# One layer of a hybrid encoder on one core: the weight sums of the output projection are made beside the first three attention steps instead of the last eight

## The chip, the core and the metric

The kernel runs on one core of one Trainium2 chip. A core has a matmul engine (TensorE, in the profile PE, with its weight loads as PEld), three engines for elementwise work (VectorE, DVE; ScalarE, ACT; GpSimd, POOL) and SyncE (SP), which issues nearly all DMAs here, in the order in which they are written. Each engine works through its own queue in order. The metric is the time of one execution in microseconds.

## What is computed

One layer works on 2048 tokens of width 1024 in float32. It has three parts, each with an RMS norm before and after and a residual: token mixing, cross-attention into 256 memory tokens, and a SwiGLU network. Token mixing is what matters here:

```python
z = u @ w_in                       # 1024 -> 2816 columns
qa, ka, va, qh, fh, ih, gh = jnp.split(z, IN_SPLITS, axis=-1)
ya = swa_with_sinks(qa, ka, va, sinks)      # sliding window attention, 8 heads
yh = hgrn2(qh, fh, ih, gh, lb, onorm)       # gated linear recurrence, 4 heads
y = jnp.concatenate([ya, yh], axis=-1) @ w_out
h = h + rms_norm(y, g_mix_post)
```

## The kernel before

**Precision.** Each float32 operand of a large product is split into a rounded high part and the rest, and a product is three matmuls (high by high, high by low, low by high; `mm3`, L156 to L158, and `products`, L1122 to L1124). The split is `split2`: the high part on ScalarE (L985) or GpSimd (L987), the low one on VectorE (L988).

**Seven products for eight.** Large products are cut into 2 x 2 blocks and made with seven block products (`seven`). For that, four sums and differences of the blocks of the moving operand are needed. For the output projection this operand is `w_out`. Its sums are made ahead of time and stored in a DRAM tensor, `out_s`, and read back as tiles `row` when the projection begins. `sums` sets that up, and the generator `combined` does it: for each of two halves of a block and for each of four keys it loads one or two blocks of `w_out` (L75, by `load`), into tiles `u` or `x` of the pool `io`, yields three times, combines them on VectorE (`put`, L1032), stores the result (L78, by `store`), and yields once more. In each half, key 5 combines an `x` into a `u`; key 7 another `x` into a new `u`, key 6 a third `x` into the same `u` once its first store has landed, and key 4 subtracts this `u` from a fourth `x`. A load of the upper rows of `w_out` takes two DMAs of 64 partitions each. There are 33 calls of `next` to the end of the generator.

**The stage around the change.** `mix` first projects the first 1024 tokens (`in_first`), and then runs three generators in turn, one step of each at a time:

- `in_proj`, L682, makes the input projection of the second 1024 tokens, one tile of 128 columns per step: 48 matmuls of 128 x 512 into banks `psg`, from weights `raw`, split into `whi` and `wlo`, with the result `z` stored to `z_d`. After the columns of a forget gate `decays` works on tiles `x` and `u` of the same pool.
- `swa` does the attention of 128 tokens per step: `swa_front` loads queries (`qd`, twice two halves), keys (`kr`) and values (`vr`) from `z_d`, splits them (`qs`, `kh` and `kl`, `vst`), multiplies (L803, L804), takes the softmax's minimum on VectorE (L808, `w_mn`), the exponential on ScalarE (L812) and scales on VectorE (L823); one step later `swa_back` transposes the result (L837), splits it (`pth`, `ptl`), multiplies by the values (L846, L847) and stores `ys` to `y_d`.
- `hgrn` does the recurrence of 128 tokens per step, in three stages over three steps, with loads `k`, `qq`, `kk`, `v` and `sg` from `z_d`; `on` (L933) is its normed output, which TensorE transposes (L941).

The first loop has nine steps (NPB + 1) with all three. The second has the remaining eight steps of `swa`, with `in_proj` but without `hgrn`, whose second half comes later, beside the products that fold the cross-attention's weights (`fold_cross`). Before the change the sums stand in this second loop: one `next` ahead of it and four per step.

**What sets the order.** The program is traced in the order of these calls; a scheduler then orders each engine's instructions from that, with its own estimate of when each could start, and pools set which tile waits for which. So a moved call also changes the order of its neighbours. Pools: `u` has 2 buffers, `x` 3, `raw` 3, `qd` 2, `kr` and `vr` 1.

Of the kernel before, what the change touches and what calls it, by code (L numbers as in the profile page):

```python
# [48 lines left out]
class Layer:  # L49
# [144 lines left out]
    def mix(self):  # L194
        tc, I = self.tc, self.I
        kw = dict(reuse_waits="tile")
        with contextlib.ExitStack() as left:
            def pool(name, at, **k):
                return at.enter_context(tc.tile_pool(name=name, bufs=1, **k, **kw))

            self.mc = pool("mc", left)
            self.r_x = self.cst.tile([P, NT], F32, name="r_x")
            with (
                tc.tile_pool(name="t1", bufs=3, **kw) as self.ts,
                tc.tile_pool(name="t2", bufs=3, **kw) as self.tb,
                tc.tile_pool(name="s1", bufs=2, side="right", **kw) as self.st_pool,
                contextlib.ExitStack() as at,
            ):
                self.banks(at, "ps1", **MOST)
                self.raws = 3  # L210
                u = self.in_first()
            self.banks(left, "ps2", **FOUR)
            self.hg = pool("hg", left)
            self.wp = pool("wp", left)
            self.io = pool("io", left)
            with tc.tile_pool(name="sw", bufs=1, side="right", **kw) as self.sw:
                self.zero_tiles()
                swa = self.swa(range(NT), lambda n: "st" if n < NPB else "sth")
                hgrn = self.hgrn(range(NPB), "h")
                cols = self.in_proj(1, u)  # L220
                next(cols)
                for _ in range(NPB + 1):
                    next(swa)
                    next(hgrn)
                    next(cols)
                for _ in hgrn:
                    pass
                self.out_sums, side = self.sums("out_s", self.w_out, 4, lambda: self.io_tile("u"), lambda: self.io_tile("x"))
                side = side()
                next(side)  # L230
                pairs = self.hgrn(range(NPB, NT), "gt")
                for i, _ in enumerate(swa, NPB + 2):
                    next(cols)
                    if i == NT + 1 - 0:
                        next(pairs)
                    for _ in range(4):
                        next(side, None)
                for _ in cols:
                    pass
            phases = self.phases(self.jobs(), None, lambda: self.io_tile("z"))  # L240
            with tc.tile_pool(name="xp", bufs=1, side="right", **kw) as self.xp:
                fold = self.fold_cross()
                for _ in range(2):
                    next(fold)
                for i, _ in enumerate(pairs, 1):
                    for _ in range(2):
                        next(fold)
                    if 2 <= i < 10:
                        next(phases)
                for _ in fold:  # L250
                    pass
            left.close()
            with (
                tc.tile_pool(name="t3", bufs=3, **kw) as self.ts,
                tc.tile_pool(name="t4", bufs=3, **kw) as self.tb,
                tc.tile_pool(name="s3", bufs=2, side="right", **kw) as self.st_pool,
                contextlib.ExitStack() as at,
            ):
                self.banks(at, "ps3", **MOST)
                self.raws = 4  # L260
                for _ in phases:
                    pass
# [1497 lines left out]
```

## Time and profile before

| what | us |
|---|---|
| median of three runs | 2584.37 |
| the three runs | 2583.25, 2584.37, 2588.23 |
| the profiled execution, as timed | 2585.97 |
| its span, first to last instruction | 2584.3 |
| first column of `in_proj` begins | 268 |
| last `out_s` store issued | 530 |
| first `out_s` read back | 782 |

The profile is one execution. An instruction's row names its line, engine, operation and tiles (out<-in, buffer numbers left out). A line can be that of a helper, so that loads are all on L75 and stores on L78; there the tile's name tells them apart. A wait row reads: who waited, on which line, for whom, the sum in us, how often, the longest. Times within the span count from its first instruction. A matmul of 512 columns is shown with some 390 ns but the next one starts before it has ended, so PE's busy time counts the union.

### The profile page before, as it was taken

What the parts mean: (1) busy time and instruction counts of PE and PEld (TensorE: products, weight loads), DVE (VectorE), ACT (ScalarE), POOL (GpSimd) and SP (SyncE); (2) the same over time, 40 slices, a digit from 0 to 9 for tenths busy, and PEclk for the clock granted to TensorE, in tenths of its full rate; (3) what the DMA queues carried; (4) which work ended last, traced back from release to release, by engine and by line L of the source; (5) the groups of instructions that cost most, each with busy time, mean ns of one, the idle gap of its engine ahead of it and who ended that gap; (6) DMA issues with size and microseconds to landing.
All of it is one profiled execution on the core that took longest, in us unless ns stands there. A gap on an engine that the chain in (4) does not pass through costs nothing.

```text
span 2584.3 us, 34943 instructions
## 1 busy us (share of the span) xinstructions
PE 2540.1 (98%) x12326; PEld 2126.7 (82%) x12326; DVE 1762.3 (68%) x2791; ACT 1262.6 (49%) x2643; POOL 427.2 (17%) x612
## 2 busy tenths in 40 slices
PE   9999999999999999999999999999999999999998
PEld 8888888878998778888778888888888888888786
DVE  7785588887556778688875655576666557564666
ACT  5563466565555566465563333344333335443543
POOL 4231334321302232212300000000000000000022
PEclk9999999999999999999999999999999999999999
DMA  6445755765887886666973622253565434576888
GB/s 188 147 163 171 203 165 159 231 193 175 245 296 278 297 278 219 217 214 205 325 245 118 207 90 74 82 204 122 182 202 186 155 109 167 180 219 173 249 223 217
DMA packets 361616, 502.10 MB, mean 194 GB/s; under 512 B 20832, under 2 KB 249184, under 8 KB 361440
## 3 DMA queue, kind: packets, MB, share of 16 engines
q1 hardware_dynamic: 355392, 477.84, 56.2%
q0 software_dynamic: 6048, 22.02, 4.7%
q8 instruction: 97, 1.59, 0.2%
q14 instruction: 79, 0.65, 0.1%
HBM read 333.07 MB, written 166.72 MB: 193 GB/s over the span
## 4 chain that ended last, share of the span: by engine, by line
PE 77%; DMA 7%; issue 6%; DVE 4%; ACT 4%; POOL 1%; SPq 1%; POOLq 0%; DVEq 0%; ACTq 0%
PE psm L1122 21%; PE psm L1123 21%; PE psm L1124 21%; PE psg L158 2%; PE psg L156 2%; PE psg L157 2%; PE pss L1381 1%; DMA row<-y_d 1%; ACT T L985 1%; DMA y_d<-sg 1%; ACT junk L1476 1%; DMA x<-in_w_out_dram 1%; DMA h1t_d<-row 1%; DMA raw<-in_wo_x_dram 0%; SPq L75 0%
## 5 line engine op out<-in xcount | busy, mean ns | idle before, releaser
L1122 PE MATMUL psm<-T,S 128*128 128x512 f32 x2680 | 1037.9, 392 | 13.5 <-ACT part L1137 7.9
L1123 PE MATMUL psm<-T,S 128*128 128x512 f32 x2680 | 1043.5, 390 | 2.3 <-DVE T L988 2.2
L1124 PE MATMUL psm<-T,S 128*128 128x512 f32 x2680 | 1031.1, 390 | 4.8 <-DVE S L988 4.8
L1122 PEld LDWEIGHTS psm<-T,S 128*128 128x128 f32 x2680 | 503.5, 188 | 124.2 <-ACT part L1137 8.8
L1124 PEld LDWEIGHTS psm<-T,S 128*128 128x128 f32 x2680 | 503.8, 188 | 111.1 <-DVE S L988 6.5
L1123 PEld LDWEIGHTS psm<-T,S 128*128 128x128 f32 x2680 | 503.9, 188 | 107.0 <-DVE T L988 4.5
L985 ACT ACTIVATE S<-sum 128x512 fp32r<-128x512 f32 (+1 forms) x330 | 198.6, 618 | 363.2 <-PE psm L1124 269.3
L988 DVE TENSOR_TENSOR S<-sraw,S 128x512 fp32r<-128x512 f32 (+1 forms) x315 | 214.2, 687 | 220.8 <-ACT S L985 206.3
L988 DVE TENSOR_TENSOR S<-sum,S 128x512 fp32r<-128x512 f32 (+1 forms) x388 | 260.3, 679 | 45.9 <-ACT S L985 30.3
L1137 ACT ACTIVATE part<-psm 128x512 f32<-128x512 f32 x285 | 168.7, 596 | 239.8 <-PE psm L1124 219.7
L985 ACT ACTIVATE S<-sraw 128x512 fp32r<-128x512 f32 (+1 forms) x268 | 165.2, 617 | 101.0 <-PE psm L1124 92.3
L1505 POOL DMA_DIRECT2D row<-y_d x28 | 25.5, 911 | 1111.1 <-DMA sraw<-hid_d 955.0
L988 DVE TENSOR_TENSOR T<-row,T 128x1024 fp32r<-128x1024 f32 (+1 forms) x112 | 132.2, 1192 | 43.9 <-ACT T L985 43.5
L1476 ACT ACTIVATE junk<-row 128x512 f32<-128x512 f32 x160 | 99.7, 624 | 60.3 <-DVE row L1498 31.2
L157 PE MATMUL psg<-u,whi 128*128 128x512 f32 x320 | 127.8, 399 | 0.0
L158 PE MATMUL psg<-u,wlo 128*128 128x512 f32 x320 | 127.1, 397 | 0.0
L156 PE MATMUL psg<-u,whi 128*128 128x512 f32 x320 | 127.0, 397 | 0.0
L985 ACT ACTIVATE T<-row 128x1024 fp32r<-128x1024 f32 (+1 forms) x112 | 113.9, 1031 | 23.6 <-DMA row<-d_s 8.5
L987 POOL TENSOR_SCALAR S<-sum 128x512 fp32r<-128x512 f32 x58 | 54.1, 934 | 296.3 <-PE psm L1124 248.5
L1642 DVE TENSOR_TENSOR row<-psm,part 128x512 f32<-128x512 f32 x66 | 43.7, 687 | 68.2 <-PE psm L1124 68.2
L1651 DVE TENSOR_TENSOR part<-psm,part 128x512 f32<-128x512 f32 x66 | 43.8, 687 | 62.9 <-PE psm L1124 62.8
L1691 DVE TENSOR_TENSOR row<-psm,part 128x512 f32<-128x512 f32 x72 | 49.0, 688 | 52.8 <-PE psm L1124 52.8
(363 smaller groups left out, 3699.7 us busy)
## 6 DMA issues: line engine op xcount, KB each, us to landing
sraw<-in_w_gate_dram SPq DMA_DIRECT2D x44, 512.0 KB, 3.7
sraw<-in_w_up_dram SPq DMA_DIRECT2D x44, 512.0 KB, 3.7
hid_d<-row SPq DMA_DIRECT2D x44, 512.0 KB, 2.7
h_d<-row SPq DMA_DIRECT2D x32, 512.0 KB, 5.0
y_d<-row SPq DMA_DIRECT2D x32, 512.0 KB, 3.3
sraw<-hid_d SPq DMA_DIRECT2D x32, 512.0 KB, 4.7
row<-y_d POOLq DMA_DIRECT2D x28, 512.0 KB, 6.3
sraw<-in_w_in_dram SPq DMA_DIRECT2D x44, 256.0 KB, 3.6
```

Of the source, the lines that this page charges most:

```text
L156: nc.tensor.matmul(ps, ah, bh, start=(i == 0), stop=False)
L157: nc.tensor.matmul(ps, ah, bl, start=False, stop=False)
L158: nc.tensor.matmul(ps, al, bh, start=False, stop=(i == n - 1))
L985: self.nc.scalar.activation(hi, raw, AF.Copy)
L987: self.nc.gpsimd.tensor_scalar(hi, raw, 1.0, 1.0, ALU.mult, ALU.mult)
L988: self.nc.vector.tensor_tensor(lo, raw, f32(hi), ALU.subtract)
L1122: nc.tensor.matmul(ps, s[:, 0, k, :], t[:, 0, k, :], start=st, stop=False, **kw)
L1123: nc.tensor.matmul(ps, s[:, 0, k, :], t[:, 1, k, :], start=False, stop=False, **kw)
L1124: nc.tensor.matmul(ps, s[:, 1, k, :], t[:, 0, k, :], start=False, stop=sp, **kw)
L1137: nc.scalar.activation(t, ps, AF.Copy)
L1476: self.nc.scalar.activation(junk, a, AF.Square, scale=float(D) ** -0.5, accum_out=to)
L1691: nc.vector.tensor_tensor(d, a, b, ALU.add)
```

## The change

The set-up of the sums and the first `next` go ahead of the first loop. In it, each step calls `next` up to eleven times, between `hgrn` and `in_proj`, so that the 33 calls are used up in the first three of the nine steps. The four calls per step in the second loop go. What is loaded, combined and stored, and in which order, is the same; so are the tiles' tags and pools.

```diff
                 cols = self.in_proj(1, u)
+                self.out_sums, side = self.sums("out_s", self.w_out, 4, lambda: self.io_tile("u"), lambda: self.io_tile("x"))
+                side = side()
+                next(side)
                 next(cols)
                 for _ in range(NPB + 1):
                     next(swa)
                     next(hgrn)
+                    for _ in range(11):
+                        next(side, None)
                     next(cols)
                 for _ in hgrn:
                     pass
-                self.out_sums, side = self.sums("out_s", self.w_out, 4, lambda: self.io_tile("u"), lambda: self.io_tile("x"))
-                side = side()
-                next(side)
                 pairs = self.hgrn(range(NPB, NT), "gt")
                 for i, _ in enumerate(swa, NPB + 2):
                     next(cols)
                     if i == NT + 1 - 0:
                         next(pairs)
-                    for _ in range(4):
-                        next(side, None)
                 for _ in cols:
                     pass
```

## The prediction, made before the changed kernel ran

> **What bounds the kernel now.** I read the page first: its first line and the row of busy times.
>
> ```profile
> span 2584.3 us, 34943 instructions
> ## 1 busy us (share of the span) xinstructions
> PE 2540.1 (98%) x12326; PEld 2126.7 (82%) x12326; DVE 1762.3 (68%) x2791; ACT 1262.6 (49%) x2643; POOL 427.2 (17%) x612
> ```
>
> TensorE is the bound: 44.2 us of 2584.3 are idle. The change adds and removes no matmul, so it can gain only TensorE idle time, and only where the sums stand now; and it can lose time only where they go. So I cut the attention part into stretches (second view: busy time by stretch; the columns are PE, PEld, DVE, ACT, POOL, granted clock, DMA share, GB/s). The first row is roughly the first three attention steps, 480 to 540 is where nearly all the sums stand today, and 540 to 600 is the same loop without them.
>
> ```profile
> core 0: us, PE busy (x) PEld busy (x) DVE busy (x) ACT busy (x) POOL busy (x), PEclk, DMA share, GB/s
> 270.00:345.00 75.00, 74.76 (x427) 64.89 (x427) 47.95 (x137) 39.33 (x129) 25.81 (x43) 1.00 0.67 191
> 345.00:440.00 95.00, 94.94 (x563) 82.65 (x562) 80.92 (x196) 63.68 (x187) 37.62 (x60) 1.00 0.52 157
> 440.00:480.00 40.00, 40.00 (x231) 34.70 (x230) 35.25 (x79) 26.63 (x67) 14.84 (x21) 1.00 0.56 161
> 480.00:540.00 60.00, 56.66 (x289) 45.56 (x287) 51.04 (x111) 32.36 (x96) 22.69 (x29) 1.00 0.98 290
> 540.00:600.00 60.00, 59.43 (x317) 49.91 (x316) 52.55 (x143) 38.54 (x111) 12.06 (x25) 1.00 0.51 155
> ```
>
> The clock is full in all of them, so it plays no part. From 270 to 480 TensorE idles 0.30 us in 210; from 480 to 540 it idles 3.34 us, with the DMA engines at 0.98; from 540 to 600, 0.57 us. The third view is who TensorE waited for from 480 to 540:
>
> ```profile
> PE psh L941 <- DVE on L933: 1.0, 1, 1.0
> PE psh L847 <- DVE ptl L842: 0.9, 2, 0.7
> PE pss L837 <- DVE w_mn L808: 0.9, 2, 0.5
> PE pst L837 <- DVE w_mn L808: 0.3, 2, 0.2
> PE psh L803 <- DVE ys L851: 0.3, 1, 0.3
> ```
>
> Always VectorE. And VectorE works in order, so I asked what VectorE itself waited for between 440 and 540, and what the chain that ended last shows there:
>
> ```profile
> DVE u L1032 <- DMA x<-in_w_out_dram: 3.1, 2, 2.0
> DVE u L1032 <- DMA out_s<-u: 2.3, 1, 2.3
> ```
>
> ```profile
> 480.37 6.49 DMA x<-in_w_out_dram
> ...
> 486.99 1.23 DVE u L1032
> ...
> 488.66 4.04 DMA x<-in_w_out_dram
> ...
> 492.76 1.22 DVE u L1032
> ```
>
> This is the whole cost of the sums today: a combination on L1032 stands in VectorE's queue before its operand has come over the full DMA engines, 5.4 us are waited, and what is queued behind it (`on`, `ptl`, the softmax minimum) reaches TensorE late.
>
> **The change, part by part.** Removed from the last eight steps and added to the first three are the same instructions: 20 loads, 8 combinations, 8 stores. Their sizes and durations:
>
> ```profile
> x<-in_w_out_dram SPq DMA_DIRECT2D x12, 256.0 KB, 5.6
> ...
> out_s<-u SPq DMA_DIRECT2D x6, 512.0 KB, 4.5
> ...
> u<-in_w_out_dram SPq DMA_DIRECT2D x4, 256.0 KB, 5.2
> ...
> u<-in_w_out_dram SPq DMA_DIRECT2D x2, 512.0 KB, 5.8
> x<-in_w_out_dram SPq DMA_DIRECT2D x2, 512.0 KB, 5.4
> out_s<-x SPq DMA_DIRECT2D x2, 512.0 KB, 6.1
> ```
>
> ```profile
> L1032 DVE TENSOR_TENSOR u<-u,x x6: 1204/1222/1226, 451.1 to 526.9; 128x1024 f32<-128x1024 f32 x6
> ...
> L1032 DVE TENSOR_TENSOR x<-x,u x2: 1207/1216/1225, 499.3 to 528.6; 128x1024 f32<-128x1024 f32 x2
> ```
>
> That is 16 x 256 + 4 x 512 KB read and 8 x 512 KB written, 10,240 KB or 10.5 MB, and 8 x 1.22 = 9.8 us of VectorE.
>
> *What goes.* Without the sums, 480 to 540 should look like 540 to 600, which runs the same work. By idle time that returns 3.34 - 0.57 = 2.8 us. By weight loads, one for each matmul, it returns more: 49.91 against 45.56, 4.35 us, which also counts matmuls that started late without a gap in the records. I take 3.3, nearer the idle time, and keep 2.8 and 4.35. [...] The trace can't settle it, since the mix of small and large matmuls in the two stretches differs (289 against 317).
>
> *What comes, on VectorE.* 47.95 + 9.8 = 57.7 of 75 us, 77%; today's stretch runs at 51.04 of 60, 85%. Nothing there is short of VectorE as such. Costing it at nothing rests on its 27 us of idle time; if an operand is late, the wait adds to it.
>
> *What comes, on the DMA engines.* 191 GB/s over 75 us are 14.3 MB; with 10.5 they are 24.8. The 290 GB/s of the fullest stretch at a share of 0.98 would need 85.5 us for it. The first three steps are short of 10.5 us of transfer time, while 480 to 540 just holds what it has. Behind them 345 to 440 runs at 157 GB/s, so what runs over finds room there, if TensorE doesn't need it before.
>
> *What comes, on SP's queue.* The first loads go ahead of the first attention step's own, which today issue back to back:
>
> ```profile
> 272.61 2.66 SPq L75 DMA_DIRECT2D qd<-z_d  x4
> ```
>
> At 2.66 / 4 = 0.67 us, four more loads issue in 2.7 us, and their 1.05 MB take 3.6 us at 290 GB/s: `qd`, `kr` and `vr` land about 3.6 us later. The order of instructions in the built program answers this: ahead of the first product that reads `kl`, 20 in-projection matmuls of the second column stand rather than 2. They start 0.22 us apart,
>
> ```profile
> 268.25 0.39 PE L157 MATMUL psm<-u,S 128*128 128x512 f32 x1
> ...
> 268.47 0.39 PE L158 MATMUL psm<-u,S 128*128 128x512 f32 x1
> ```
>
> so 18 x 0.22 = 4.0 us cover the 3.6. In steps two and three that cover is mostly missing: the score matmuls stand where they stood, give or take a few matmuls, with x and u loads of the sums and two `out_s` stores ahead of their `qd` and `kr` on SP. Each store waits on SP for its combination, and all behind it with it. In VectorE's order a combination stands right ahead of the first softmax minima of step one, and the second of each chain waits for the store of the first, as the 2.3 us row shows today. What is queued behind are `qs`, `vst`, `wlo` and the scaled `S`, and TensorE waits for these.
>
> No row shows sums beside steps with their own HGRN work, so the cost is bounded from both sides: at nothing, since TensorE idles 0.24 us there now and the order may cover the rest; at 10.5 us, if the whole overrun reaches TensorE. Nearest is today's stretch: 3.34 us for the 7 combinations that start in it (all but the one at 451.1), so 8/7 x 3.34 = 3.8. I take 3.8: VectorE has more room, the DMA engines less.
>
> [...] Loads already wait behind the sums where they meet; SP has one queue. By the DMA issues of 440 to 545 and of 270 to 345, a load of `kk` took 8.2 us to land beside the sums, and 4.3 in the first steps:
>
> ```profile
> kk<-z_d SPq DMA_DIRECT2D x1, 256.0 KB, 8.2
> ```
>
> ```profile
> kk<-z_d SPq DMA_DIRECT2D x4, 256.0 KB, 4.3
> ```
>
> [...]
>
> *The readers of the sums* start long after either place:
>
> ```profile
> L75 SPq DMA_DIRECT2D row<-out_s x8: 319/352/668, 781.6 to 803.6; - x8
> ```
>
> **The sum.** -3.3 + 3.8 = +0.5 us. The profiled execution took 2585.97 us (its span of 2584.3 and 1.67 around it), so 2586.5 for such a one; the median of the three runs is 1.6 us lower, 2584.37, so **2584.9 us**.
>
> **Rivals.** (1) *Slower: the DMA engines become the bound of the first three steps.* Place: `qd`, `kr` and `k` of steps two and three, behind the sums on SP. Price: up to the 10.5 us overrun, less the lower gain of 2.8, so +7.7: 2592.1 us. It decides once TensorE feels more than 3.3 + 5.2 = 8.5 us of the 10.5. For it: the 0.67 that is already there, landings of 8.2 us under load, a written order that can't step aside. Against it: room behind at a share of 0.52, and in today's full stretch TensorE lost only 3.34 of 60 us with the DMA engines at 0.98.
>
> (2) *Faster: the first steps hide it all.* Place: the idle 27 us of VectorE and the covered first step. Cost nothing, gain 4.35: 2580.0 us. For it: TensorE idles 0.24 us there, and the instruction order has moved products back. Against it: the overrun. Even this is 0.17% and stays within what can be told; to be faster by more, the new order of the remaining steps would have to save further time, of which the 0.63 us idle in 345 to 440 and 540 to 600 leave little.
>
> (3) *The change doesn't do what it says*, because the scheduler puts the sums back. The built order excludes it: all eight `out_s` stores stand ahead of the first `y_d<-sg` store on SP, where now they come after the fifth. I give it nothing.
>
> **How the numbers follow.** Forecast 0.58, rival 1 0.30, rival 2 0.12. About 0.2%, 5.2 us, is what a measurement of this kernel can tell from no change. The forecast lies within it at all but its edge; rival 1 lies mostly beyond it, and takes with it the slow edge of the forecast, 0.32; of rival 2 half is given to a gain beyond it, 0.06; that leaves 0.62. The range goes from rival 2's time to rival 1's, 2580 to 2592; as rival 1's price takes the whole overrun, most of its weight lies below that end.
>
> **What would show it.** Right: 480 to 540 with TensorE idle under 1 us and a DMA share near 0.5; the first three steps with a share above 0.9 and TensorE idle 3 to 5 us, its waits naming VectorE and VectorE's naming L1032. The slower rival: TensorE idle 8 us or more before 360, waits of `qs`, `kl` or `atz` for DMA of `z_d`, landings of `qd` near 8 us. The hidden case: idle under 1 us in both places. Wrong altogether: a loss or gain after 600, in the hand-over to the next stage, which I leave as it is.

## The result, and the profile after

The changed kernel took **2600.44 us** (median of 6 runs, 2595.68 to 2606.16), the kernel before on the same chip 2587.74 (6 runs, 2583.25 to 2588.47): a ratio of 1.0058, 95% interval 1.0045 to 1.0070. It is slower by 12.7 us by the medians and by 15.0 by the ratio, which is worked out from all runs; +0.5 was predicted, and the time lies above the range. The profiled execution took 2600.87 us; its page begins:

```profile
span 2599.2 us, 34961 instructions
## 1 busy us (share of the span) xinstructions
PE 2545.1 (98%) x12326; PEld 2130.9 (82%) x12326; DVE 1767.2 (68%) x2791; ACT 1258.9 (48%) x2643; POOL 427.6 (16%) x612
```

TensorE idles 54.1 us instead of 44.2, and its 12,326 matmuls take 5.0 us more busy time. That already says that idle time alone won't explain 14.9 us of span: matmuls ran slower somewhere. The attention stretches by busy time (PE, PEld, DVE, ACT, POOL, granted clock, DMA share, GB/s), as in the prediction:

```profile
270.00:345.00 75.00, 69.15 (x368) 57.83 (x367) 47.08 (x120) 30.46 (x103) 22.45 (x33) 1.00 1.05 280
345.00:440.00 95.00, 91.09 (x537) 78.57 (x536) 79.95 (x185) 60.84 (x179) 40.54 (x61) 1.00 0.58 171
...
480.00:540.00 60.00, 59.75 (x325) 50.47 (x324) 51.77 (x124) 35.77 (x102) 20.70 (x31) 1.00 0.48 149
```

The place that the sums left is as predicted: from 480 to 540 the idle time falls to 0.25 us at a DMA share of 0.48. The place that they went to isn't: TensorE idles 5.85 us in the first row and 3.91 in the second, 9.8 in all (7.1 of it before 360), with a DMA share of 1.05 in the first row. Who waited there, TensorE from 270 to 440 and then VectorE from 270 to 345:

```profile
PE pst L847 <- DVE ptl L842: 2.8, 2, 1.6
PE pss L784 <- DMA vr<-z_d: 2.6, 2, 1.5
PE psh L911 <- DVE sg L942: 1.7, 1, 1.7
PE pst L803 <- DVE qs L769: 1.2, 1, 1.2
```

```profile
DVE u L1032 <- DMA x<-in_w_out_dram: 15.7, 2, 11.1
```

VectorE stands 15.7 us at L1032, three times what it did before. But one of TensorE's four long waits is for a load of the attention itself, `vr`. And ScalarE, which makes the high part of `qs`, stands 7.7 us for `qd` from 270 to 345, where before it stood 3.6:

```profile
ACT qs L768 <- DMA qd<-z_d: 7.7, 4, 2.9
```

The loads of 270 to 345 (KB each, median us to landing), before and after, show why:

```profile
qd<-z_d SPq DMA_DIRECT2D x24, 128.0 KB, 3.3
...
vr<-z_d SPq DMA_DIRECT2D x5, 64.0 KB, 2.7
```

```profile
qd<-z_d SPq DMA_DIRECT2D x19, 128.0 KB, 6.7
...
vr<-z_d SPq DMA_DIRECT2D x4, 64.0 KB, 4.3
```

To see where the 14.9 us lie, two rows of each kernel are enough: the first and last start of the attention columns' first product (L156), and of the projection's (L1122). Before, then after:

```profile
L156 PE MATMUL psg<-u,whi x320: 387/390/527, 268.7 to 627.9; 128*128 128x512 f32 x160
L1122 PE MATMUL psm<-T,S x2536: 388/389/651, 778.0 to 2574.5; 128*128 128x512 f32 x196
```

```profile
L156 PE MATMUL psg<-u,whi x320: 387/392/532, 272.7 to 640.5; 128*128 128x512 f32 x160
L1122 PE MATMUL psm<-T,S x2536: 387/389/628, 796.1 to 2589.4; 128*128 128x512 f32 x196
```

The attention takes 367.8 us (640.5 - 272.7) where it took 359.2: **+8.6**. The hand-over, from the last column to the projection, takes 155.6 where it took 150.1: **+5.5**. Ahead of the attention 4.0 are lost (272.7 against 268.7), and behind 796.1 3.2 are won (2599.2 - 796.1 against 2584.3 - 778.0); nothing is changed in these two, and both vary from run to run. 4.0 + 8.6 + 5.5 - 3.2 = 14.9.

Of the 5.5 us in the hand-over, 2.8 are idle time of TensorE (9.11 against 6.34 us) and 2.7 busy time. The two hand-overs, before and after:

```profile
627.90:778.00 150.10, 143.76 (x1097) 136.14 (x1096) 79.78 (x113) 84.50 (x194) 33.57 (x44) 1.00 0.85 271
640.50:796.10 155.60, 146.49 (x1090) 138.61 (x1089) 79.46 (x111) 83.15 (x192) 32.45 (x43) 0.97 0.82 259
```

After the change two waits follow each other from 640 to 660, first for `z` and then for `vt`, and the clock is halved from 647 to 657:

```profile
PE pst L923 <- ACT vt L902: 3.1, 1, 3.1
PE psg L884 <- DVE z L711: 1.9, 1, 1.9
```

```profile
640.00:647.00 7.00, 5.08 (x37) 4.56 (x36) 3.55 (x5) 4.43 (x7) 0.00 (x0) 1.00 0.59 137
647.00:657.00 10.00, 6.92 (x32) 6.57 (x31) 4.48 (x8) 3.17 (x12) 0.79 (x1) 0.50 1.03 280
```

ScalarE's own order (start, us, and the idle time before it) shows why `vt` was late: it stood behind a high part of the projection's first operand, which waited for rows of `w_out`.

```profile
650.75 1.06 ACT L985 ACTIVATE T<-z 128x1024 fp32r<-128x1024 f32 x1 [3.78 <-DMA z<-in_w_out_dram]
651.71 0.58 ACT L902 ACTIVATE vt<-pst 128x512 f32<-128x512 f32 x1
```

### The profile page after: what moved, and what is told of

Its sections match the earlier page's. It is cut to its first block, busy times and chain, and to the rows that moved or that the text cites. A ratio compares the mean times of both kernels' runs of the same rounds, so it can differ in the third digit from the quotient of the medians.

```text
span 2599.2 us, 34961 instructions
## 1 busy us (share of the span) xinstructions
PE 2545.1 (98%) x12326; PEld 2130.9 (82%) x12326; DVE 1767.2 (68%) x2791; ACT 1258.9 (48%) x2643; POOL 427.6 (16%) x612
## 4 chain that ended last, share of the span: by engine, by line
PE 82%; DMA 7%; DVE 4%; ACT 3%; issue 2%; POOL 1%; SPq 0%; DVEq 0%; POOLq 0%; ACTq 0%
PE psm L1122 22%; PE psm L1124 22%; PE psm L1123 22%; PE psg L158 2%; PE psg L156 2%; PE psg L157 2%; PE pss L1381 1%; DMA row<-in_w_down_dram 1%; ACT T L985 1%; DVE S L988 1%; DMA u<-in_w_out_dram 1%; DMA u_d<-row 0%; DMA raw<-in_wv_x_dram 0%; DMA z<-in_w_out_dram 0%; DVE T L988 0%
## 5 line engine op out<-in xcount | busy, mean ns | idle before, releaser
L1122 PE MATMUL psm<-T,S 128*128 128x512 f32 x2680 | 1037.8, 392 | 15.2 <-ACT part L1137 11.0
L1122 PEld LDWEIGHTS psm<-T,S 128*128 128x128 f32 x2680 | 503.9, 188 | 124.8 <-ACT part L1137 13.1
L988 DVE TENSOR_TENSOR S<-sraw,S 128x512 fp32r<-128x512 f32 (+1 forms) x315 | 214.9, 689 | 229.0 <-ACT S L985 213.1
L988 DVE TENSOR_TENSOR S<-sum,S 128x512 fp32r<-128x512 f32 (+1 forms) x388 | 260.9, 680 | 45.4 <-ACT S L985 29.9
L1137 ACT ACTIVATE part<-psm 128x512 f32<-128x512 f32 x285 | 168.8, 596 | 243.7 <-PE psm L1124 223.6
L988 DVE TENSOR_TENSOR T<-row,T 128x1024 fp32r<-128x1024 f32 (+1 forms) x112 | 132.4, 1193 | 40.7 <-ACT T L985 40.2
L156 PE MATMUL psg<-u,whi 128*128 128x512 f32 x320 | 128.2, 401 | 0.0
L985 ACT ACTIVATE T<-row 128x1024 fp32r<-128x1024 f32 (+1 forms) x112 | 114.2, 1033 | 23.2 <-DMA row<-d_s 12.7
L1691 DVE TENSOR_TENSOR row<-psm,part 128x512 f32<-128x512 f32 x72 | 49.0, 688 | 54.0 <-PE psm L1124 52.2
```

What stands on the lines that cost most here:

```text
L156: nc.tensor.matmul(ps, ah, bh, start=(i == 0), stop=False)
L985: self.nc.scalar.activation(hi, raw, AF.Copy)
L988: self.nc.vector.tensor_tensor(lo, raw, f32(hi), ALU.subtract)
L1122: nc.tensor.matmul(ps, s[:, 0, k, :], t[:, 0, k, :], start=st, stop=False, **kw)
L1137: nc.scalar.activation(t, ps, AF.Copy)
L1691: nc.vector.tensor_tensor(d, a, b, ALU.add)
```

## The experiments

Three questions: is the attention's loss due to the DMA engines' bytes, SP's queue or VectorE's combinations; what does removing the sums gain by itself; and what lengthens the hand-over. In the table the attention and the hand-over are read from the two rows named above in each run's profile (us; the hand-over's us at half clock beside it), each time from one execution, and the runs are compared with runs of the kernel before on the same chip, whose medians were 2584.68 to 2587.74. The ratio is worked out from all of these runs, so it need not be the quotient of two medians.

| kernel | median us | ratio to before, 95% | attention | hand-over (at half clock) |
|---|---|---|---|---|
| before | 2587.74 | 1 | 359.2 | 150.1 (0) |
| after | 2600.44 | 1.0058, 1.0045 to 1.0070 | 367.8 | 155.6 (10.2) |
| e1_spread9 | 2593.70 | 1.0031, 1.0020 to 1.0042 | 364.6 | 155.3 (3.4) |
| e2_mid3 | 2594.04 | 1.0030, 1.0017 to 1.0042 | 365.5 | 156.7 (3.4) |
| e3_late3 | 2589.50 | 1.0013, 1.0004 to 1.0023 | 361.9 | 153.2 (3.4) |
| e4_no_combine | 2594.14 | 1.0042, 1.0025 to 1.0059 | 367.4 | 158.0 (6.8) |
| e5_quarter | 2594.17 | 1.0036, 1.0024 to 1.0048 | 362.9 | 158.5 (13.7) |
| e6_tail4 | 2588.74 | 1.0013, 0.9997 to 1.0028 | 358.0 | 155.9 (3.4) |
| e7_no_sums | 2595.69, one run | - | 356.0 | 156.8 (6.8) |
| e8_before_again | 2582.20, one run | - | 358.8 | 150.1 (0) |
| e9_quarter_no_combine | 2592.49 | 1.0025, 1.0014 to 1.0036 | 360.6 | 158.0 (3.4) |
| e10_spread17 | 2592.71 | 1.0019, 1.0007 to 1.0030 | 365.4 | 153.5 (3.4) |
| e11_after_pool_split | 2596.30 | 1.0033, 1.0021 to 1.0045 | 369.7 | 154.5 (6.8) |
| e12_before_pool_split | 2588.93 | 1.0004, 0.9995 to 1.0013 | 356.4 | 156.9 (10.2) |
| e13_poolq_quarter | 2590.55 | 1.0014, 1.0001 to 1.0027 | 356.1 | 155.4 (6.8) |
| e14_poolq | 2606.76 | 1.0083, 1.0052 to 1.0114 | 375.5 | 153.8 (3.4) |

The same code twice (before and e8) differs by 0.4 us in the attention and by nothing in the hand-over; e11, whose edit lies behind the attention, differs there from after by 1.9. Smaller differences between two rows show nothing.

**Other places for the sums.** Four calls beside each of the nine steps:

```diff
-                    for _ in range(11):
+                    for _ in range(4):
```

> The sums spread over the first nine steps, 4 calls of next per step, rather than 11 in each of the first three. Theory (transfers): the changed kernel lost its time because 10.5 MB more had to pass in 75 us that had room for 7; over 190 us at a DMA share of 0.67 to 0.52 there is room for 20 MB, so the stage should lose little, 0 to 3 us, while the 3 to 4 us of 480 to 540 come back: 2582 to 2588 us beside 2587.7 of before. Rival (VectorE's order): eight combinations in an in-order queue cost the same wherever they stand beside steps with recurrence work, since VectorE is at 85% in 345 to 440: 2595 to 2600 us.

```profile
270.00:345.00 75.00, 69.70 (x377) 58.25 (x376) 50.02 (x130) 32.53 (x107) 20.53 (x35) 1.00 1.02 259
```

Spreading the calls hardly spread the loads: the first stretch is still full (1.02) and TensorE still idles 5.30 us there. Only the second stretch is better: there it idles 1.33 us rather than 3.91. Then steps four to six:

```diff
-                next(side)
...
-                for _ in range(NPB + 1):
+                for step in range(NPB + 1):
...
-                    for _ in range(11):
+                    for _ in range(11 if step > 2 else 0):
```

> As concentrated as the changed kernel (11 calls in each of three steps), but in steps four to six rather than one to three. Theory (transfers): the DMA engines are at 0.52 there, not 0.67, so the overrun is 24.8 less 3.5 MB, nearly nothing over 75 us: loss of 3 to 6 us instead of 12, 2588 to 2594 us. Rival (VectorE's order): VectorE is busier there (85% against 64%), so the loss is as large or larger: 2600 us or more.

The DMA share is 0.88 and 0.72 in the two stretches, TensorE idles 3.71 and 4.41 us, and the attention takes 365.5 us. It isn't the test that was meant: the scheduler drew nine of the twenty loads forward, to 276 to 301, and issued the other eleven from 359 to 389. From 270 to 310 the share is 1.02 and TensorE idles 3.40 us, as in the runs before; behind the second batch (0.93 from 355 to 395) it idles another 3.44 us from 395 to 440. So the loss does not need all the loads in the first three steps, and more isn't shown. The first three steps of the second loop, and its last four, both as edits of the kernel before:

```diff
-                    for _ in range(4):
+                    for _ in range(11):
```

> 11 calls per step in the first three steps of the second loop, where before has 4 per step in eight. Concentration alone, at the old place without recurrence work. Theory (transfers): the DMA share without the sums is about 0.5 there, so the loss is that of before (3 to 4 us) to twice it: 2586 to 2593 us. Rival (VectorE's order): the same 8 combinations in less time beside the forget gates' scans, VectorE above 95% for 60 us, loss of 8 us or more: 2592 to 2600 us.

```diff
-                next(side)
...
-                    for _ in range(4):
+                    for _ in range(8 if i > NT - 3 else 0):
```

> The other direction: 8 calls per step in the last four of the second loop's eight steps, so that the sums run into 540 to 620, where the DMA share is 0.5 and then 0.2. Theory (bytes): less crowding than before, the 3.3 us of 480 to 540 shrink, 2582 to 2587 us, unless the sums run into the hand-over to the next stage, whose DMA share is 0.91: then 2588 us or more. Rival (VectorE's order): 8 combinations at 88% busy cost as before or more, 2587 to 2590 us.

Both lie near the kernel before (1.0013 each), with the attention at 361.9 and 358.0 us. They load the same stretch, 480 to 540, at a share of 0.97 and 1.03. Against no sums (356.0, below) that is 5.9 and 2.0 us, so beside these steps, which have no recurrence of their own, the same bytes cost less. And two calls beside each of all seventeen steps:

```diff
-                    for _ in range(11):
+                    for _ in range(2):
...
+                    for _ in range(2):
+                        next(side, None)
```

> The sums advanced by two calls beside every attention step of both loops, the same work as in both kernels. Theory (the first columns lose by the DMA engines' time and by VectorE standing for loads, and the steps of 480 to 540 us lose 3 to 4 us where the sums stand in the kernel before): spread this thin the sums cost neither, the DMA share stays under 0.8 from 270 to 600, the attention columns take 357 to 361 us (360.3 before, 368.1 after, 356.5 without sums), the hand-over goes as its order falls out, and the total is 2583 to 2590. Rival: the scheduler draws the loads forward into the first columns as it did with four calls a step (share 1.02 from 270 to 345), TensorE idles 4 us or more there, and the total is 2592 or more.

The theory fell: with a share of only 0.89 and 0.60 in the first two stretches, TensorE idles 3.61 and 3.86 us in them. Again nine loads went out early, from 275 to 306; from 270 to 310 the share is 1.00, and all of the 3.6 us are lost there. A share below 1 over a long stretch doesn't mean that loads are in time within it.

**What the sums cost at all.** No sums in the attention; the projection makes them when it begins, so the total isn't comparable:

```diff
-                self.out_sums, side = self.sums("out_s", self.w_out, 4, lambda: self.io_tile("u"), lambda: self.io_tile("x"))
-                side = side()
-                next(side)
+                self.out_sums, side = None, iter(())
```

> No sums ahead of the projection at all; the output projection makes them itself from the blocks, so the total time is not comparable, but the attention steps and the hand-over show the floor. Theory (bytes): the first eight columns lose what they lose in before (7.5 us, 3 of it in the first four), and 480 to 540 idles under 1 us. Rival (the new order alone): any other order than the one of before loses 10 us or more in the first eight columns.

Its two rows (its later lines are two lower):

```profile
L156 PE MATMUL psg<-u,whi x320: 387/390/527, 271.2 to 627.2; 128*128 128x512 f32 x160
L1120 PE MATMUL psm<-T,S x2536: 387/389/797, 784.0 to 2584.3; 128*128 128x512 f32 x196
```

The attention takes 356.0 us. So the sums cost 359.2 - 356.0 = **3.2 us** where they stood, and 367.8 - 356.0 = **11.8 us** where they went. The hand-over takes 156.8 us, with the same two waits as after and no sums ahead of it: it isn't lengthened by what the sums do in their new place. To see how much is chance, the kernel before once more, with no edit:

> The kernel before once more, for its hand-over. If the half clock of 10 us at 647 in the changed kernel is chance, one may be seen here as well; if it follows from the TensorE waits of the changed hand-over, 620 to 660 shows a full clock and idle time near 3.1 us again.

Its hand-over is 150.1 us again, without half clock and with 6.40 us of idle time (6.34 in the first). So before's hand-over isn't luck of one execution; it goes with that order of instructions.

**What the 11.8 us are made of.** The eight combinations left out, so that the stored sums are single blocks:

```diff
...
-                with self.behind():
-                    nc.vector.tensor_tensor(t, t, o, op)
+                if dst is not self.out_dst:
+                    with self.behind():
+                        nc.vector.tensor_tensor(t, t, o, op)
```

> The changed kernel with all of its loads and stores in the first three steps, but the 8 combinations on VectorE left out: out_s holds single blocks in place of their sums and differences. Theory (transfers): the same 10.5 MB in the same place, so nearly the same loss, 2596 to 2601 us; TensorE goes on waiting for vr, qs and kl. Rival (VectorE's order): nothing in VectorE's queue waits for a weight block, so the loss goes: 2582 to 2588 us.

The attention still takes 367.4 us. TensorE's longest total wait from 270 to 345 is now the load itself:

```profile
PE pss L784 <- DMA vr<-z_d: 3.7, 3, 1.6
```

VectorE's 15.7 us of standing were not the main cause. By the two profiles they are worth 0.4 us, less than the 1.9 us of e11, and the execution profiled here took 2602.31 us, 8.2 more than the median of its kernel. By the totals they may be worth some 4 us (1.0042 against 1.0058, with intervals that overlap); most of the loss stays, but the median of 2594.14 us lies below the 2596 of the theory as well. Next, the same transfers and combinations with 32 of 128 partitions each; the rest of the sums is left out, and plain rows of `w_out` are read in its stead:

```diff
...
-            src(t, i, j, k0, n)
-            return t
+            (src_part if name == "out_s" else src)(t, i, j, k0, n)
+            return t[0:32] if name == "out_s" else t
```

> The changed kernel with the same loads, combinations and stores in the same three steps, each on 32 partitions rather than 128: the same number of instructions, the same waits, a combination that takes as long, but a quarter of the bytes, 2.6 of 10.5 MB (the other partitions of the sums are left out, and plain weights read in their place). Theory (bytes through the DMA engines): the share of 270 to 345 falls from 1.05 to about 0.8, TensorE's lost time up to the eighth column from 20 us (issue gaps included; 7.5 before) to 8 to 11 us, total 2584 to 2591 us. Rival (number and order of DMAs on SP): 20 loads and 8 stores still stand ahead of qd, kr and vr, so loss and time stay: 17 us or more, 2593 us or more.

The attention takes 362.9 us: 4.9 of the 11.8 go with the bytes, and the long waits for `vr` with them. The total stays where the rival, number and order of the transfers, had it (2594.17, where it asked for 2593 or more). Both edits together:

> The changed kernel with both suspects of the first columns taken away at once: the sums' transfers carry 32 of 128 partitions, and VectorE's eight combinations are left out (the stored rows are parts of single blocks of the matrix; the rest of the operand is read from the matrix where the projection loads it). The transfers' number, their place beside the first three attention steps and their place in SP's queue stay. Theory: either suspect alone holds TensorE there, the bytes by late landings, the combinations by VectorE standing in order for a load, and this is why neither run with one of them removed got the time back; with both gone TensorE idles under 2 us in all from 270 to 440 us (9.8 in the changed kernel, 0.3 in the one before), and the first eight attention columns take 149 to 152 us (162.9 after, 148.9 before). The hand-over behind 630 us stays long, so the total is 2586 to 2592. Rival: the number of transfers queued on SP, or the scheduler's new order of the attention steps, costs the time: TensorE idles 5 us or more there, the first eight columns stay at 157 or more, and the total at 2593 or more.

The attention takes 360.6 us, 4.6 above no sums, and the first eight columns, of sixteen L156 matmuls each, 153.7: between what theory and rival gave. What stays isn't combinations, and with a DMA share of 0.76 from 270 to 345 it is no overrun of bytes. SyncE's issues (start, us of issuing) show what else there is:

```profile
295.77 0.49 SPq L75 DMA_DIRECT2D x<-in_w_out_dram  x1
296.32 0.88 SPq L75 DMA_DIRECT2D u<-in_w_out_dram  x2
297.25 0.89 SPq L75 DMA_DIRECT2D x<-in_w_out_dram  x2
301.19 0.32 SPq L78 DMA_DIRECT2D out_s<-x  x1
301.63 0.36 SPq L78 DMA_DIRECT2D out_s<-u  x1
302.04 0.42 SPq L75 DMA_DIRECT2D u<-in_w_out_dram  x1
302.51 0.90 SPq L75 DMA_DIRECT2D x<-in_w_out_dram  x2
303.45 1.24 SPq L75 DMA_DIRECT2D qd<-z_d  x2
```

SyncE issues these in the order shown. The first store waits for the tile that it writes out, and here that takes 3.0 us, until 301.2, in which nothing is issued. The query rows `qd` are issued at 303.45, behind eight loads and two stores of the sums, and ScalarE, which turns them into `qs`, waits:

```profile
SPq L78 <- DMA x<-in_w_out_dram: 3.0, 1, 3.0
```

```profile
ACT qs L768 <- DMA qd<-z_d: 6.3, 2, 4.5
```

So the same small transfers on GpSimd's queue, as an edit of the run before (what is left out stays left out):

```diff
-                self.store(dst[self.CHAIN.index(key), 0:t.shape[0],
+                (nc.gpsimd.dma_start if dst is self.out_dst else self.store)(dst[self.CHAIN.index(key), 0:t.shape[0],
...
-                self.load(t[m * s:m * s + m], self.I["w_out"]
+                self.nc.gpsimd.dma_start(t[m * s:m * s + m], self.I["w_out"]
```

> The run before with a quarter of the partitions and no combinations, with one more edit: the sums' loads and stores are issued by GpSimd on its own queue instead of SyncE (what is left out stays left out). Theory (SyncE's queue, which holds about eight transfers in flight, makes the load of the query rows wait behind the sums' loads): the 4.8 us that stay in the first eight columns (153.7 us, 148.9 before) go, to 148.5 to 150.5, and TensorE idles under 1.5 us from 270 to 440 us. Rival (the scheduler's new order, or the engines' time for small transfers): 152 us or more. GpSimd issues 22 transfers itself, which may delay its own chain; then the waits of TensorE name GpSimd's tiles.

The attention takes 356.1 us, as without sums, and TensorE idles 2.0 us from 270 to 440, where under 1.5 was expected. The first eight columns took 144.5, less than the 148.5 to 150.5 expected; part of their work moved behind them, so that the whole attention is what to compare. The 4.5 us went with SyncE's queue. How exact that size is, isn't shown: the edit gave the scheduler a new order as well, a new order alone moved the attention by 2.8 us (e12 against before, below), and the totals of the two runs have intervals that overlap. With full transfers on GpSimd's queue:

> The changed kernel whole, with the sums' loads and stores issued by GpSimd on its own queue instead of SyncE. Theory (three parts: bytes, VectorE's standing for the loads, SyncE's queue): only the queue's part goes, so the first eight columns fall from 162.9 us by at most 5, to 157 to 161, with the DMA share still over 0.95 from 270 to 345, and the total is 2594 to 2600. Rival (SyncE's queue is the whole of it, as the attention's loads stand behind the sums'): 152 or less, the total 2590 or less. Other rival (a second queue lets more of the sums' bytes in at once, ahead of the attention's loads): 164 or more, 2602 or more.

```profile
270.00:345.00 75.00, 60.00 (x302) 50.22 (x302) 37.31 (x100) 25.79 (x87) 31.65 (x54) 0.92 1.00 255
```

```profile
PE pss L784 <- DMA vr<-z_d: 9.7, 2, 5.4
```

```profile
q1 hardware_dynamic: 16675, 10.11, 57.5%
q0 software_dynamic: 2575, 8.91, 42.2%
```

The slowest of all, and the other rival was right: on a queue of their own the sums' bytes came in beside the attention's (42.2% of the engines' time against 57.5%), `kk` took 11.6 us to land (5.7 in after), TensorE waited up to 5.4 us at once for `vr`, and the granted clock was 0.92 from 270 to 345.

**The hand-over.** The eight high parts that ScalarE waits with, on GpSimd instead (1.20 us each there, 1.06 on ScalarE); only the hand-over's order is meant to change. On after, then on before:

```diff
-            phases = self.phases(self.jobs(), None, lambda: self.io_tile("z"))
+            self.by, phases = "P", self.phases(self.jobs(), None, lambda: self.io_tile("z"))
...
-            self.split2(t, dst[:, 0, a:b], dst[:, 1, a:b], "A")
+            self.split2(t, dst[:, 0, a:b], dst[:, 1, a:b], self.by)
```

> The changed kernel with one edit that acts in the hand-over alone: the eight high parts of the projection's first operands (ScalarE 1.06 us each, waiting there 17.6 us in all for the matrix's rows) are made on GpSimd (1.15 us for the same shape). Theory of the hand-over: ScalarE stands in order for those rows with the transposed values of the pair's step queued behind it, and TensorE waits 3.1 us for them at 649 us, with a half-clock stretch behind; with the wait on GpSimd the stretch from the fold's first product to the projection's first falls from 148.5 us to 144 or less, and the total by 3 to 7 us against the changed kernel (2600.4). Rival: the hand-over's length comes from the order of TensorE's own instructions or from the transfers, which this leaves: 147 to 150 us, and the total within 2 us of the changed kernel.

> The kernel before with the same one edit in the hand-over. Theory: there ScalarE waits 12.5 us for the same rows, but what stands behind it is needed later, and TensorE's own waits are for a load of v and for the fold's high part; so little is gained, 135 to 139 us for the stretch from the fold to the projection (138.7 before), total 2582 to 2587. Rival: the scheduler's other order of the hand-over costs as it does in all the variants so far, and the stretch takes 144 us or more, the total 2589 or more.

On after the wait for `vt` goes, and the next one grows, from 1.9 to 3.6 us:

```profile
PE psg L884 <- DVE z L711: 3.6, 1, 3.6
```

The stretch from the fold to the projection falls from 148.5 to 145.5 us, not to 144; the hand-over keeps 154.5 of its 155.6. ScalarE's wait was one link and not the cause. On before the same edit lengthens the hand-over to 156.9 us, and the stretch from the fold to the projection from 138.7 to 146.1: the rival was right. Yet its attention takes 356.4 us, without any change to the sums:

```profile
480.00:540.00 60.00, 59.10 (x303) 48.20 (x302) 54.61 (x124) 34.28 (x102) 22.16 (x30) 1.00 0.95 293
```

0.9 us of idle time where before has 3.34, at nearly the same DMA share: what the sums cost in their old place depends on the order around them, too, and the total is unchanged (1.0004). No version beat the kernel before beyond its interval.

## Why the prediction was wrong

- **The gain was right.** Predicted 3.3 (2.8 to 4.35), measured 3.2 (before against e7), or 2.8 with e8 in before's place. Its signs hold as well: idle under 1 us, a share near 0.5. The size holds for before's order only; in that of e12 the sums cost 0.4 at the same place.
- **The price of the new place was the step that failed.** "Nearest is today's stretch: 3.34 us for the 7 combinations that start in it", so 8/7 x 3.34 = 3.8. Measured: 11.8, above even the upper bound of 10.5. The row was scaled by combinations, and by the profiles those are worth 0.4 (e4) to 2.3 (e9 against e5). From one run to the next: small transfers on another queue +0.1 (e7 to e13), SyncE's queue +4.5 (e13 to e9), bytes +6.8 (e9 to e4), combinations +0.4 (e4 to after), in sum 11.8. Each is a difference of two executions, to which the order alone can add 1.9 to 2.8 (e11, e12). e5 gives the other order: bytes 4.9, combinations 2.3, of which some 1.5, an estimate, go with e5's granted clock of 0.98 over the 75 us from 270 (1.00 in e9). Today's stretch has full DMA engines (0.98), but they just carry what they have, beside steps that load nothing for the recurrence; it could not show an overrun.
- **"VectorE has more room"** was true and worth nothing. That TensorE's waits would name VectorE and VectorE's would name L1032 came true as well, which is the trap: `qs` was late with its load (ScalarE stood 7.7 us for `qd`, and 19.9 without combinations), and without combinations most of the loss stayed.
- **The cover of step one** (18 matmuls, 4.0 us against 3.6) reckoned with four loads ahead, issued back to back; in the run `kr` was issued one landing at a time. At its end TensorE waits for `vr`, and the loss goes on to 440. "Room behind at a share of 0.52" didn't help either: 3.91 us are lost there.
- **Rival 1 was the right mechanism**, at the place that it named, `qd` and `vr` behind the sums on SP, though its sign was just missed (7.1 us of idle time before 360, where it asked for 8; 9.8 by 440; landings of `qd` 6.7 us, where it asked for some 8). Its evidence was all in the prediction: 85.5 us of transfers in 75, and `kk` 8.2 us under load. Its price at the new place, the whole overrun of 10.5, was the nearest to the 11.8 measured. But the price has two parts, and the queue's would stay with no overrun.
- **The hand-over was left out.** "Wrong altogether: a loss or gain after 600, in the hand-over to the next stage, which I leave as it is": 5.5 us are lost there, 2.8 by idle time and 2.7 by busy time, with 10.2 us at half clock. With no sums ahead of it at all it is 156.8. It is 153.2 or more in every order but before's, even with one edit that concerns only the hand-over itself. So it isn't lost to the moved sums' transfers or to the readers of `out_s`. That the scheduler's other order is the reason is what is left. Which choice of the scheduler makes before's order better stays open; the one link that was tried (e11) gave way to the next.

With the measured terms the sum is -3.2 + 11.8 + 5.5 = +14.1 by the profiles, against +12.7 by the medians.

## What to carry to other kernels

When work moves, price its transfers by the bytes that the new stretch has to carry and by what stands behind them in the issuing queue (here 6.8 and 4.5 us), not by what the moved operations cost at their old place. A wait of an engine on a moved operation is no proof that the operation is the cause: leave it out and see whether the loss goes. With a scheduler that orders the whole stage anew, a later stretch can lose as much as the edit gains (here 5.5 us against 3.2); give that a term and a width of its own.

## What the runs showed of the hardware

- Ahead of their last 10 us, the clock granted to TensorE in before and in after was 0.50 for stretches of 3.4, 6.8 or 10.2 us. In before 1.8 us of waiting (`part`, L1137) came ahead of 3.4 us at 0.50 from 966.8. In the changed kernel 1.9 us of waiting (`z`, L711) came ahead of 10.2 us at 0.50, with the 3.1 us for `vt` inside them. In e14 two waits for `vr`, of 5.4 and 4.3 us, are each followed by 3.4 us at 0.50; the rows are the first of these and the 3.4 us behind it:

```profile
282.30:287.90 5.60, 0.35 (x2) 0.00 (x0) 0.49 (x1) 1.02 (x2) 0.00 (x0) 1.00 0.88 183
288.00:291.40 3.40, 3.39 (x9) 2.72 (x10) 3.24 (x5) 0.62 (x2) 1.91 (x3) 0.50 0.37 112
```

- Waits of nearly the same length were followed by half clock or not. In the kernel before TensorE waits 2.4 us for `S` (L988) until 892.4, and the clock is 1.00 from there to 900; it waits 2.3 us for `row` (L1691) until 2420.1, and 3.4 us at 0.50 follow from 2420.9.
- What a half-clock stretch costs shows as busy time, on top of the idle time ahead of it: in after the products of 128 x 512 start 0.43 us apart from 157 to 161, at 0.50, and 0.23 apart from 150 to 152, at 1.00, so that about half of what TensorE is busy within a stretch is added. Ahead of its last 10 us before has three such stretches of 3.4 us, after 6.8, 10.2 and 3.4. TensorE is busy for 9.9 us of these in before and for 16.7 in after; half of the 6.8 us between them, an estimate, is 3.4 of the 5.0 us by which PE's busy time grew. Where the rest lies isn't shown.
- SyncE had at most eight transfers in flight in before and in after. In after the last of the four `qd` and what follows were issued one landing at a time: the fourth `qd` at 282.1, when the `sg` issued eight transfers earlier had landed, the first `kr` at 283.4, when the first `x` had, the second at 284.7 and `vr` at 285.8, when the two `u` had, though none of them reads or overwrites what these bring. The rows are the issues (start, us until the group is issued) and what SyncE waited for from 270 to 345:

```profile
276.08 0.51 SPq L75 DMA_DIRECT2D sg<-z_d  x1
276.63 0.73 SPq L75 DMA_DIRECT2D x<-in_w_out_dram  x1
277.41 1.27 SPq L75 DMA_DIRECT2D u<-in_w_out_dram  x2
278.72 0.60 SPq L75 DMA_DIRECT2D x<-in_w_out_dram  x1
279.37 3.29 SPq L75 DMA_DIRECT2D qd<-z_d  x4
283.42 1.85 SPq L75 DMA_DIRECT2D kr<-z_d  x2
```

```profile
SPq L75 <- DMA x<-in_w_out_dram: 6.3, 9, 1.4
```

  So the `sg`, `x` and `u` ahead, which took 6.0 to 7.8 us to land, also delayed the issue of the fourth `qd`, of `kr` and of `vr`.
